# Attention in a fused two-layer encoder: scores with the sign turned, their minimum seeded with minus the sink, the sink as one more column under the exponential

## The chip, the cores and the metric

The kernel runs on one core of one Trainium2 chip. The time is the device time of one execution in microseconds (us), and of several runs the median is given. The engines are named as in the profile: PE is the matrix engine (PEld its weight loads), DVE the vector engine, ACT the scalar engine, POOL the GpSimd engine, SP the queue that issues the DMAs.

## What is computed

The reference is an encoder of two layers over two sequences, 256 and 512 tokens long, of width 1024. Layer 0 mixes tokens with an mLSTM, layer 1 with sliding-window attention; each is followed by a gated feed-forward with a short convolution. The part that matters here is the attention of layer 1: 16 query heads in 4 key/value groups, head width 64, query blocks of 128 and a window of 128 on each side, a bias per head that depends on the distance, and a learned sink per head, which takes part in the softmax as one more score without a value:

```python
s = einsum('bqkgd,bckd->bkgqc', qb, kb) * scale + bias
s = where(valid, s, -inf)
m = maximum(max(s, axis=-1, keepdims=True), sink)
p = exp(s - m)
denom = sum(p, axis=-1, keepdims=True) + exp(sink - m)
ob = einsum('bkgqc,bckd->bqkgd', p / denom, vb)
```

## The kernel before, in words

All 768 tokens lie side by side. A matrix product is made of three passes with operands split into a high and a low part (`whi`, `wlo` for weights, `zh`, `zl` for activations); ACT writes the high part (L259), DVE the low one (L260). Weights arrive by DMA in pieces of 512 KB into the tile `raw` (L268).

The attention is the function `swa`. First the keys and the first queries are projected (`window`), then the values (`gemmN`). `queries` (L876) takes a projected query tile out of the accumulator: ACT writes the high part times 0.125 (L887), DVE the low part (L888). The bias rows of all heads come from one small product; ACT copies it to the tile `bs` (L899), and it goes through memory (`brow`), from where each head's bias tile `bt` is fetched (L962).

Then comes the loop over 48 blocks (L1033). A block is one pair of heads by one query block of 128 rows; it sees two or three key tiles, K = 256 or 384 columns (32 blocks of the first kind, 16 of the second). Each step of the loop has four kinds of work:

- `project` (L915): a few matmuls of the remaining query projections, and later of the output projection, as filler;
- `scores` (L955) of block x: for each of the two heads (index e) PE multiplies queries and keys into an accumulator bank from the rotation `pa` of four; DVE adds the bias, writes the sum to the tile `t` and takes its maximum in the same instruction (L978). On 128x2 operands DVE then takes the maximum with the sink (L983), the sink minus that maximum (L984) and the negated maximum (L985). ACT makes the exponential of each head with its sum (L987), and the exponential of the sink's difference (L990). DVE adds the two (L991) and inverts the sum (L992); POOL multiplies the probabilities by the result (L994);
- `flip` (L996) of block x-3 (LAG is 3): PE transposes the probabilities into `pa` (L1002), ACT (L1006) and DVE (L1004) copy them to the tile `pt`;
- `values` (L1008), for three blocks at once: PE multiplies by the values, and when a sequence is complete the output is split into its two parts.

`t` has four buffers, `pt` five, `bt` three. The order on PE is as the loop is written (`manual_schedule` for PE alone, L1032). The order on DVE, ACT, POOL and SP is chosen when the program is built, by a timed model of the program; each engine then works through its queue in that order.

Of the kernel before, what the change touches and what calls it, by code (L numbers as in the profile page):

```python
# [10 lines left out]
F32 = mybir.dt.float32  # L11
R = mybir.dt.float32r
AF = mybir.ActivationFunctionType
ALU = mybir.AluOpType

P = 128
# [26 lines left out]
BIG = 1.0e30  # L43
# [9 lines left out]
SK = FG + 8  # L53
# [113 lines left out]
class Net:  # L167
# [679 lines left out]
    def swa(self, pool):  # L847
        nc, io = self.nc, self.io
# [27 lines left out]
        def queries(u, c):  # L876
            if c == 0:
                qts[u] = self.slab([P, 4, T], R)
            qt = qts[u]

            def evac(q, o):
                s0, s1 = SEQS[q]
                for e in range(2):
                    src = o[64 * e : 64 * e + 64]
                    hi = qt[64 * e : 64 * e + 64, 2 * c + e, s0:s1]
                    lo = qt[64 - 64 * e : 128 - 64 * e, 2 * c + e, s0:s1]
                    nc.scalar.activation(hi, src, AF.Copy, scale=0.125)  # L887
                    nc.vector.scalar_tensor_tensor(lo, src, 0.125, hi.bitcast(F32), ALU.mult, ALU.subtract)  # L888

            return evac  # L890

# [4 lines left out]
        pb = self.pa()[0:16]  # L896
        self.mm(pb, rb, oh, True, True)
        bs = pool.tile([16, 512], F32, tag="t", name="bs", bufs=4)
        nc.scalar.copy(bs, pb)  # L899

        bd = self.dp.tile([16, 512], F32, name="brow")
        nc.sync.dma_start(bd, bs)
# [39 lines left out]
        for j in range(8):  # L942
            for q, (s0, s1) in enumerate(SEQS):
                n = (s1 - s0) // P
                for i in range(n):
                    b = Block()
# [5 lines left out]
        bias = {}  # L952
        po = {}

        def scores(b):  # L955
            j, kv = b.j, b.j // 2
            if j not in bias:
                bias[j] = []
                for e in range(2):
                    bt = pool.tile([P, 384], F32, tag="bt", name=self.nm("bt"), bufs=3)  # L960
                    row = bd[2 * j + e : 2 * j + e + 1]
                    nc.sync.dma_start(  # L962
                        bt, bass.AP(tensor=row.tensor, offset=row.offset, ap=[[1, P], [1, 384]])
                    )
                    bias[j].append(bt)
            co = (b.lo - b.i + 1) * P
            k0 = b.s0 + b.lo * P
            q0 = b.s0 + b.i * P
            K = b.K
            b.t = t = pool.tile([P, 2, 384], F32, tag="t", name=self.nm("t"), bufs=4)  # L970
            st = pool.tile([P, 8], F32, tag="st", name=self.nm("st"), bufs=6)
            rm, mx, sm, rd = (st[:, 2 * z : 2 * z + 2] for z in range(4))
            for e in range(2):
                S = self.pa()[:, :K]
                qb = qts[j // 2][:, 2 * (j % 2) + e, q0 : q0 + P]
                for z in range(2):
                    self.mm(S, qb, kk[kv // 2][:, kv % 2, z, k0 : k0 + K], z == 0, z == 1)
                nc.vector.tensor_tensor_reduce(  # L978
                    out=t[:, e, :K], in0=S, in1=bias[j][e][:, 384 - co - K : 384 - co][:, ::-1], op0=ALU.add, op1=ALU.max,
                    scale=1.0, scalar=-BIG, accum_out=rm[:, e : e + 1],  # L980
                )
            sk = self.cst(SK + 2 * j, 2)
            nc.vector.tensor_tensor(mx, rm, sk, ALU.max)  # L983
            nc.vector.tensor_tensor(rd, sk, mx, ALU.subtract)  # L984
            nc.vector.tensor_scalar(mx, mx, -1.0, None, ALU.mult)  # L985
            for e in range(2):
                nc.scalar.activation(  # L987
                    t[:, e, :K], t[:, e, :K], AF.Exp, bias=mx[:, e : e + 1], accum_out=sm[:, e : e + 1]
                )
            nc.scalar.activation(rd, rd, AF.Exp)  # L990
            nc.vector.tensor_tensor(rd, rd, sm, ALU.add)  # L991
            nc.vector.reciprocal(rd, rd)  # L992
            for e in range(2):
                nc.gpsimd.tensor_scalar(t[:, e, :K], t[:, e, :K], rd[:, e : e + 1], 1.0, ALU.mult, ALU.mult)  # L994

# [36 lines left out]
        with self.tc.manual_schedule(engines={mybir.EngineType.PE}):  # L1032
            for x in range(nb + LAG + 1):  # L1033


                while done < min(113, AHEAD + (x + 1) * (113 - AHEAD) // 40) + max(0, 14 * (x - 40) // 10):
                    next(fill, None)
                    done += 1
                if x < nb:
                    scores(blocks[x])  # L1040
                if LAG <= x < nb + LAG:
                    flip(blocks[x - LAG])
                if x > LAG and (x - LAG) % GROUP == 0:
                    for b in blocks[x - LAG - GROUP : x - LAG]:
                        values(b)
# [620 lines left out]
```

## Time and profile before

| what | value |
|---|---|
| median of three timed runs | 1853.66 us (1852.61 to 1855.81) |
| span of the profiled execution, first to last instruction | 1851.5 us |
| total of the profiled execution beside its span | not listed; the median of the timed runs stands 2.16 us above the span |
| mean granted clock of PE over the span | 0.989 |
| DVE busy over the span | 1394.5 us (75%) |
| ACT busy over the span | 897.3 us (48%) |
| POOL busy over the span | 475.3 us (26%) |
| first and last bias-and-maximum on DVE (L978) | 1095.9 and 1237.9 us into the span |

Busy time says how long an engine had an instruction in work; it doesn't say that anybody waited for it. A view of waits names, for an engine that sat idle, what ended the idle time. The chain of work that ended last is followed back from the last instruction, so its shares tell what set the end. A view by windows gives the busy time of each engine in a stretch of the span, in the order PE, PEld, DVE, ACT, POOL, then the granted clock, the DMA share and the DMA rate.

### The profile page before, as it was taken

The page shows a single profiled execution, that of the slowest core. Times are in us where ns is not written, and L with a number is a line of the kernel's source. Part 1 is how long each engine was busy: PE and PEld are TensorE (multiplying, and loading weights), DVE is VectorE, ACT ScalarE, POOL GpSimd, SP SyncE. Part 2 cuts the span into 40 slices and gives each one's busy share as a digit, 9 for nine tenths or more (in the row PEclk, how much of TensorE's full clock was granted, in tenths as well). Part 3 has the DMA queues.
Part 4 walks back from the last instruction along what each step waited for, and adds up shares of the span by engine and source line. Part 5 has one row for each costly group of instructions (what it writes and reads, how often), then busy time and mean ns, then how long its engine had stood idle before and what let it go on. Part 6 is the DMA issues. An engine that isn't in the chain of part 4 may idle for free.

```text
span 1851.5 us, 29083 instructions
## 1 busy us (share of the span) xinstructions
PE 1799.6 (97%) x11290; PEld 1660.0 (90%) x11290; DVE 1394.5 (75%) x2292; ACT 897.3 (48%) x1815; POOL 475.3 (26%) x386
## 2 busy tenths in 40 slices
PE   6999999999999999999999999999999999999997
PEld 3987887888998999999999898889989999999997
DVE  4755676886689777777877858876898777777876
ACT  4444443443456444444444546765564444444443
POOL 1001001021024333333331313330134333333322
PEclk7999999999999999999999999999999999999999
DMA  8343556546312222222222321123122222222212
GB/s 329 117 147 132 174 190 223 168 139 201 106 46 80 69 69 69 68 69 69 68 69 83 104 82 49 52 94 121 51 92 69 69 69 69 69 69 69 69 35 69
DMA packets 64246, 184.49 MB, mean 100 GB/s; under 512 B 6167, under 2 KB 23831, under 8 KB 64108
## 3 DMA queue, kind: packets, MB, share of 16 engines
q1 hardware_dynamic: 64108, 182.63, 30.1%
q8 instruction: 89, 1.46, 0.3%
q14 instruction: 49, 0.40, 0.1%
HBM read 176.17 MB, written 6.43 MB: 99 GB/s over the span
## 4 chain that ended last, share of the span: by engine, by line
PE 86%; DVE 6%; DMA 3%; ACT 2%; issue 1%; POOL 1%; SPq 0%; POOLq 0%; ACTq 0%; DVEq 0%
PE ps L253 27%; PE pa L253 25%; PE ps L1163 10%; PE ps L1166 10%; PE ps L1164 10%; PE pa L1002 1%; DMA raw<-in_adaln_w_dram 1%; DVE wlo L260 1%; DMA raw<-in_w_dram 1%; DVE slab L589 1%; DMA slab<-in_adaln_w_dram 1%; PE pa L1166 0%; PE pa L1164 0%; PE pa L1163 0%; DMA slab<-mrows 0%
## 5 line engine op out<-in xcount | busy, mean ns | idle before, releaser
L259 ACT CAST whi<-raw 128x1024 fp32r<-128x1024 f32 x237 | 248.0, 1048 | 344.8 <-PE pa L253 162.0
L260 DVE TENSOR_TENSOR wlo<-raw,whi 128x1024 fp32r<-128x1024 f32 x237 | 322.3, 1361 | 113.7 <-ACT whi L259 111.7
L253 PE MATMUL pa<-slab,whi 128*128 128x256 f32 (+1 forms) x1472 | 346.5, 331 | 3.2 <-DVE slab L589 3.2
L253 PEld LDWEIGHTS pa<-slab,whi 128*128 128x128 f32 x1472 | 252.7, 188 | 27.5 <-DVE slab L589 4.6
L589 DVE SCALAR_TENSOR_TENSOR slab<-pa,mod,slab 128x256 f32<-128x256 f32 (+1 forms) x368 | 211.4, 593 | 69.6 <-PE pa L253 69.3
L253 PE MATMUL pa<-slab,wlo 128*128 128x256 f32 (+1 forms) x736 | 233.8, 330 | 0.0
L253 PE MATMUL ps<-zh,whi 128*128 128x256 f32 (+1 forms) x560 | 188.9, 338 | 2.3 <-ACT whi L259 1.7
L253 PE MATMUL ps<-zh,wlo 128*128 128x256 f32 (+1 forms) x560 | 184.1, 330 | 2.1 <-DVE wlo L260 2.1
L253 PE MATMUL ps<-zl,whi 128*128 128x256 f32 (+1 forms) x560 | 185.0, 332 | 0.0
L1163 PE MATMUL ps<-zh,whi 128*128 128x384 f32 x504 | 172.2, 342 | 3.7 <-ACT nt L1234 1.9
L1164 PE MATMUL ps<-zl,whi 128*128 128x384 f32 x504 | 169.9, 337 | 0.8 <-DVE zl L1120 0.8
L1166 PE MATMUL ps<-zh,wlo 128*128 128x384 f32 x504 | 168.9, 335 | 0.0
L253 PEld LDWEIGHTS pa<-slab,wlo 128*128 128x128 f32 x736 | 138.5, 188 | 13.1 <-DVE wlo L260 0.4
L1199 POOL TENSOR_TENSOR raw<-raw,raw 128x512 f32<-128x512 f32 x40 | 52.0, 1301 | 330.5 <-DVE wlo L260 246.1
L253 PE MATMUL ps<-slab,whi 128*128 128x384 f32 x512 | 132.2, 339 | 2.2 <-ACT sg L841 1.3
L1396 POOL TENSOR_TENSOR slab<-slab 128x772 f32<-128x772 f32 x44 | 86.5, 1967 | 171.5 <-DVE slab L1384 159.6
L1383 DVE SCALAR_TENSOR_TENSOR slab<-slab,cstt,slab 128x771 f32<-128x771 f32 x88 | 105.4, 1199 | 26.6 <-ACT slab L1381 26.4
L253 PEld LDWEIGHTS ps<-zh,whi 128*128 128x128 f32 x560 | 107.4, 192 | 15.9 <-issue 4.4
L505 DVE SCALAR_TENSOR_TENSOR ada<-raw,silc,ada 128x1024 f32<-128x1024 f32 x84 | 109.0, 1335 | 14.3 <-DMA raw<-in_adaln_w_dram 14.0
L253 PEld LDWEIGHTS ps<-zh,wlo 128*128 128x128 f32 x560 | 107.2, 192 | 12.4 <-DVE wlo L260 3.1
L253 PEld LDWEIGHTS ps<-zl,whi 128*128 128x128 f32 x560 | 107.2, 192 | 11.9 <-issue 3.4
L1196 POOL TENSOR_TENSOR raw<-raw 128x512 f32<-128x512 f32 x40 | 61.0, 1525 | 199.2 <-DMA raw<-in_w_dram 171.0
(294 smaller groups left out, 4303.0 us busy)
## 6 DMA issues: line engine op xcount, KB each, us to landing
raw<-in_w_dram SPq DMA_DIRECT2D x208, 512.0 KB, 3.7
raw<-in_adaln_w_dram SPq DMA_DIRECT2D x84, 512.0 KB, 4.6
slab<-in_x_dram SPq DMA_DIRECT2D x12, 512.0 KB, 7.1
slab<-in_adaln_w_dram SPq DMA_DIRECT2D x12, 512.0 KB, 10.3
slab<-mrows SPq DMA_DIRECT2D x8, 384.0 KB, 5.5
xs<-slab SPq DMA_DIRECT2D x6, 512.0 KB, 3.7
bt<-brow SPq DMA_DIRECT2D x16, 192.0 KB, 3.0
slab<-xs SPq DMA_DIRECT2D x6, 512.0 KB, 6.6
```

The source lines that it names most:

```text
L253: self.nc.tensor.matmul(out, lhsT, rhs, start=start, stop=stop)
L259: nc.scalar.copy(hi, src)
L260: return nc.vector.tensor_tensor(lo, src, hi.bitcast(F32), ALU.subtract)
L505: stt(acc[:, s], row, w, acc[:, s], ALU.mult, ALU.add)
L589: self.nc.vector.scalar_tensor_tensor(x, o, self.mod[l][:, gc + c, q : q + 1], x, ALU.mult, ALU.add)
L1163: mm(o, wh[:, k], hi[k], start=start and k == 0, stop=False, skip_group_check=True)
L1164: mm(o, wh[:, k], lo[k], start=False, stop=False, skip_group_check=True)
L1166: mm(o, wl[:, k], hi[k], start=False, stop=k == 3, skip_group_check=True)
L1196: tt(q[2], q[2], q[3], ALU.add)
L1199: tt(q[0], q[2], q[0], ALU.subtract)
L1383: stt(y[:, 1:], u[:, :-1], w(0), y[:, 1:], ALU.mult, ALU.add)
L1396: nc.gpsimd.tensor_tensor(y, y, yrow[:, j], ALU.mult)
```

## The change

The queries are scaled by -0.125 instead of 0.125, and the bias rows are negated as they are copied to `bs`, so every masked score comes out with the sign turned. A new tile `nsk` holds minus the sinks of all 16 heads; one DVE instruction fills it. The instruction that adds the bias now takes the minimum, and starts it from minus the sink of its head, read from `nsk` (before, it started from a constant). The result is minus the maximum that the softmax needs, so the three small DVE instructions go. `t` grows from 384 to 386 columns per head; ACT writes minus the sink into column K of both heads, and each exponential, with scale -1, runs over K + 1 columns. Its sum contains the sink's share, so the separate exponential and the addition go. Only the reciprocal is left of the small instructions.

```diff
-                    nc.scalar.activation(hi, src, AF.Copy, scale=0.125)
-                    nc.vector.scalar_tensor_tensor(lo, src, 0.125, hi.bitcast(F32), ALU.mult, ALU.subtract)
+                    nc.scalar.activation(hi, src, AF.Copy, scale=-0.125)
+                    nc.vector.scalar_tensor_tensor(lo, src, -0.125, hi.bitcast(F32), ALU.mult, ALU.subtract)
...
-        nc.scalar.copy(bs, pb)
+        nc.scalar.activation(bs, pb, AF.Copy, scale=-1.0)
+        nsk = pool.tile([P, 16], F32, name="nsk")
+        nc.vector.tensor_scalar(nsk, self.cst(SK, 16), -1.0, None, ALU.mult)
...
-            b.t = t = pool.tile([P, 2, 384], F32, tag="t", name=self.nm("t"), bufs=4)
-            st = pool.tile([P, 8], F32, tag="st", name=self.nm("st"), bufs=6)
-            rm, mx, sm, rd = (st[:, 2 * z : 2 * z + 2] for z in range(4))
+            b.t = t = pool.tile([P, 2, 386], F32, tag="t", name=self.nm("t"), bufs=4)
+            nc.scalar.copy(t[:, :, K : K + 1], nsk[:, 2 * j : 2 * j + 2].unsqueeze(2))
+            st = pool.tile([P, 6], F32, tag="st", name=self.nm("st"), bufs=6)
+            low, sm, rd = (st[:, 2 * z : 2 * z + 2] for z in range(3))
...
-                    out=t[:, e, :K], in0=S, in1=bias[j][e][:, 384 - co - K : 384 - co][:, ::-1], op0=ALU.add, op1=ALU.max,
-                    scale=1.0, scalar=-BIG, accum_out=rm[:, e : e + 1],
+                    out=t[:, e, :K], in0=S, in1=bias[j][e][:, 384 - co - K : 384 - co][:, ::-1], op0=ALU.add, op1=ALU.min,
+                    scale=1.0, scalar=nsk[:, 2 * j + e : 2 * j + e + 1], accum_out=low[:, e : e + 1],
                 )
-            sk = self.cst(SK + 2 * j, 2)
-            nc.vector.tensor_tensor(mx, rm, sk, ALU.max)
-            nc.vector.tensor_tensor(rd, sk, mx, ALU.subtract)
-            nc.vector.tensor_scalar(mx, mx, -1.0, None, ALU.mult)
             for e in range(2):
                 nc.scalar.activation(
-                    t[:, e, :K], t[:, e, :K], AF.Exp, bias=mx[:, e : e + 1], accum_out=sm[:, e : e + 1]
+                    t[:, e, : K + 1], t[:, e, : K + 1], AF.Exp, bias=low[:, e : e + 1], scale=-1.0,
+                    accum_out=sm[:, e : e + 1],
                 )
-            nc.scalar.activation(rd, rd, AF.Exp)
-            nc.vector.tensor_tensor(rd, rd, sm, ALU.add)
-            nc.vector.reciprocal(rd, rd)
+            nc.vector.reciprocal(rd, sm)
```

## The prediction

> **What bounds the kernel now.** The page's chain of the work that ended last comes first, because it tells which engine sets the end at all.
>
> ```profile
> PE 86%; DVE 6%; DMA 3%; ACT 2%; issue 1%; POOL 1%; SPq 0%; POOLq 0%; ACTq 0%; DVEq 0%
> ```
>
> PE holds 86% of it. Everything that the change takes away belongs to DVE and ACT, so it can shorten the run only where PE waits for those two. The change touches one stage, the 48 blocks of attention. I cut that stage by windows at the places where PE's busy time falls short of the stretch.
>
> ```profile
> 1095.00:1100.00 5.00, 5.00 (x38) 4.91 (x37) 3.91 (x15) 3.14 (x7) 0.00 (x0) 1.00 0.14 52
> 1100.00:1107.00 7.00, 5.50 (x33) 4.17 (x32) 6.34 (x32) 6.60 (x23) 2.82 (x6) 1.00 0.27 77
> 1107.00:1217.00 110.00, 109.99 (x920) 98.01 (x918) 94.90 (x387) 75.77 (x248) 35.37 (x71) 1.00 0.16 47
> 1217.00:1225.00 8.00, 5.61 (x39) 4.20 (x36) 6.67 (x31) 6.12 (x23) 2.08 (x4) 1.00 0.30 91
> 1225.00:1250.00 25.00, 24.46 (x227) 22.78 (x228) 15.03 (x69) 12.78 (x45) 7.89 (x16) 1.00 0.38 127
> ```
>
> The second number is the length, the third PE's busy time. In 110 us of the middle PE is busy for 109.99, though DVE is at 94.90 there: a crowded engine, but nobody on PE waits for it. PE's idle time is 1.50 us in the second row, 2.39 in the fourth, 0.54 in the last, 0.01 in the third: **4.44 us in all, and that is the ceiling** of what a faster softmax can bring here. PE's waits in the same stretch name what it waited for:
>
> ```profile
> PE pa L1002 <- POOL t L994: 1.9, 3, 1.2
> PE pa L1002 <- DVE st L983: 1.3, 1, 1.3
> PE ps L253 <- DVE slab L260: 0.5, 1, 0.5
> PE pa L1002 <- DVE pt L1004: 0.5, 1, 0.5
> ```
>
> Three of the four rows are transposes (L1002) that come before their probabilities are ready, or before a bank is free. The 0.5 us for L260 is the split of the last output, which the change doesn't touch.
>
> **The change part by part.** First the small instructions, counted in the stage (busy us, then mean ns):
>
> ```profile
> L984 DVE TENSOR_TENSOR st<-cstt,st 128x2 f32<-128x2 f32 x48 | 11.8, 246 | 1.1
> L985 DVE TENSOR_SCALAR st<-st 128x2 f32<-128x2 f32 x48 | 10.1, 209 | 0.9
> L983 DVE TENSOR_TENSOR st<-st,cstt 128x2 f32<-128x2 f32 x48 | 9.3, 194 | 0.1
> L991 DVE TENSOR_TENSOR st<-st 128x2 f32<-128x2 f32 x48 | 7.8, 163 | 7.9 <-ACT t L987 7.5
> L990 ACT ACTIVATE st<-st 128x2 f32<-128x2 f32 x48 | 9.6, 201 | 27.9 <-DVE st L984 27.6
> L987 ACT ACTIVATE t<-t,st 128x384 f32<-128x384 f32 x32 | 19.4, 611 | 0.6 <-DVE st L985 0.3
> ```
>
> Removed from DVE: 11.8 + 10.1 + 9.3 + 7.8 = 39.0 us busy. Removed from ACT: 9.6 us. Added to ACT: 48 copies of 128x2. No such copy is in the trace; the nearest row is the removed exponential itself, 201 ns on the same shape, so 48 x 0.20 = 9.6 us, and ACT comes out even (the bounds are nothing and 0.4 us each, twice the row; I take the row). The extra column is one element of 385: 611 / 384 = 1.6 ns at most, 96 times, 0.15 us.
>
> The minimum now starts from a value per partition. Whether that costs anything for this instruction no row shows, but another DVE instruction stands in the trace in both forms, with a column of values (L589) and with a constant (L263), on the same shape:
>
> ```profile
> L589 DVE SCALAR_TENSOR_TENSOR slab<-pa,mod,slab 128x512 f32<-128x512 f32 x160 | 116.5, 742 | 25.3 <-PE pa L253 25.3
> L263 DVE SCALAR_TENSOR_TENSOR slab<-ps,slab 128x512 fp32r<-128x512 f32 x8 | 5.5, 686 | 2.0 <-ACT slab L262 2.0
> ```
>
> 742 - 686 = 56 ns. I take that estimate, with nothing and twice that as bounds: 96 x 0.056 = 5.4 us on DVE. Net, DVE loses about 34 us of its 126.85 in the stage. Within the 110 us of the middle this is worth **nothing**, because PE already runs there without a wait. The cover for that statement is PE's own work; it would be gone only if a new wait came in (below).
>
> Once each, ahead of the loop: the fill of `nsk` (about 0.2 us on DVE, the row of L985) and the sign of `bs`, a copy that stays a copy. The first scores come tens of us behind them; DVE may hold PE up by that 0.2 us at most. The sign of the queries changes no instruction. The wider `t` puts the second head 8 bytes off its old place; no row isolates that, and I take nothing (bounds: 0.05 us either way per instruction, on engines with slack). No DMA is added, moved or resized.
>
> What is left is the two bubbles. The chain of work, read inside them, shows whose time they are. The first:
>
> ```profile
> 1100.56 0.16 DVE st L991
> 1100.72 0.07 DVE st L984
> ...
> 1101.34 0.07 DVE st L985
> ...
> 1101.74 0.30 DVE st L983
> ...
> 1102.38 0.11 DVE st L984
> ...
> 1103.63 0.07 DVE st L983
> 1103.70 0.09 DVE st L985
> ...
> 1105.13 0.59 POOL t L994
> ...
> 1105.76 0.55 PE pa L1002 x3
> ```
>
> All DVE rows here are instructions that go: 0.16 + 0.07 + 0.07 + 0.30 + 0.11 + 0.07 + 0.09 = 0.87 us. Four bias instructions stand between them and get longer: 4 x 0.056 = 0.22. Saved: 0.65 us. The second:
>
> ```profile
> 1218.56 0.07 DVE st L983
> 1218.63 0.07 DVE st L991
> ...
> 1219.65 0.07 DVE st L984
> ...
> 1221.54 0.17 DVE st L985
> ...
> 1222.04 0.07 DVE st L983
> ...
> 1222.45 0.07 DVE st L984
> 1222.53 0.46 DVE pt L1004
> 1222.99 0.15 DVE st L985
> 1223.14 0.07 DVE st L991
> ```
>
> The small ones are 0.74 us, less 0.22 for four longer bias instructions: 0.52. The copy L1004 (0.46) lies in this chain only because the negation that ACT waits for stands behind it in DVE's queue; without the negation ACT may start when the bias instruction ends. Saved: 0.98 us. Together **1.6 us**, to which the end of the stage adds nothing: its wait is for a split that stays. When the small instructions are gone, what is late next is DVE's long work in the same chain: weight splits, copies, the bias instructions.
>
> The profiled execution would go from 1851.5 us of span to 1849.9. Nothing outside the span changes. The median of the runs shown is 1853.66, 2.16 above that span, so the sum makes 1852.1.
>
> One rule speaks against reading PE's busy time as I did. The Trainium skill, page "Perfetto Trace Analysis", section "Identifying the Most-Contended Engine", holds matmul busy time to be a bad measure, since matmuls are pipelined, and would have the share of weight loads read instead. By it the middle stretch would have 110 - 98.01 = 12 us of room, and the sum could be 12 us lower; the trace speaks against it, since no wait of PE's falls into that stretch.
>
> **The rivals.** (1) *The bubbles stay.* The order on DVE and ACT is made anew by the builder's model, and a long instruction may again stand ahead of a late transpose. For it: the long rows in both chains remain. Against: DVE gets a quarter of its load off. Time: 1853.7, or a few us more with a new bubble of the size of the second (2.39).
>
> ```profile
> L978 DVE CUSTOM_DVE_ANT_0 t<-pa,bt x96: 404/425/560, 1095.9 to 1237.9; 128x256 f32<-128x256 f32 x64, 128x384 f32<-128x384 f32 x32
> ```
>
> (2) *Slower: ACT's copy waits for a buffer.* The copy is the first writer of a `t` buffer. There are four, so for block x it must wait until PE has transposed block x-4. Before, DVE's bias instruction was that writer, and its scores came from PE after those transposes anyway. Now the wait stands in ACT's in-order queue, and behind it are exponentials and the copies that free banks for PE. One block ahead it costs nothing. It decides from the point where the builder puts the copy three blocks ahead of an exponential: then each block must run, one after the other, PE's transposes, the copy 0.20, two exponentials with their sums 2 x 0.61 + 0.19, POOL's first head 0.59, transposes 2 x 0.55. With 0.16 for the reciprocal (as L991) that is 3.5 us, for three key tiles, against a pitch of 3.0 (the row above: 48 blocks from 1095.9 to 1237.9, 142 / 47). 16 such blocks x 0.45 = 7 us: 1861. For it: the copy waits for no scores, so it can be placed early. Against: a model that knows of the buffer would not place it there, and ACT has room (75.77 of 110).
>
> (3) *The change doesn't stop at the bubbles.* If PE in the middle is held by something that the waits don't show, 12 us more could go, as worked out above: 1840. Against it: 109.99 of 110.
>
> **How the numbers follow.** Forecast 0.55, alone 1849 to 1853.5 (between the ceiling and almost nothing). Rival (1) 0.18, rival (2) 0.22, rival (3) 0.05. About 0.2%, here 3.7 us, is what a measurement of this kernel can tell from no change. Faster by more: rival (3) and the part of the forecast in which nearly all 4.44 us go, 0.05 + 0.13 = 0.18. Slower by more: rival (2) and the worst of (1), 0.22 + 0.03 = 0.25. Within: 0.57. The range goes from the ceiling with the scatter of the runs (1853.66 - 4.44 - 1.2), 1848, up to rival (2) at 1861; it leaves out rival (3) and about half of (2), some 0.16.
>
> **What would show it.** Right: the middle of the stage as full on PE as before; DVE's busy time in the stage down by about 34 us with the run hardly shorter; the bias instruction's median near 480 ns (425 before); waits for L994 and for DVE at the transposes down from 3.7 us to about 2. Wrong: PE waits inside the middle stretch; ACT idle before the copy of the sink with PE's transposes named; bias instructions that wait for that copy; a bubble at the start or near the end longer than 2.4 us.

## The result, and the profile after

The changed kernel took 1847.27 us in the median of seven runs (1845.5 to 1852.27), the kernel before, run beside it, 1854.77 (seven runs, 1849.79 to 1857.39). The ratio is 0.9966, with a 95% interval from 0.9952 to 0.998. The gain is 7.5 us where I had 1.6, and by more than the 0.2% that a measurement of this kernel can tell from no change. My forecast of 1852.1 was 4.8 us too high, the time lies 0.7 us below my range, and to "faster by over 0.2%" I had given 0.18.

The profiled execution has a span of 1843.8 us instead of 1851.5. PE issues the same 11,290 matmuls in the same order in both kernels, so matmul n of one trace can be set against matmul n of the other, and the starts tell where the 7.7 us went, counted from the first matmul: 2.4 are gained ahead of the attention stage, 6.4 in it, 1.1 are given back at the start of the next feed-forward. In the twelve other kernels below, the part ahead of the stage differs from before by anything from -2.7 to +1.8 us, although their code there is the same but for a sign and the fill of `nsk`, so this part scatters (1.1 of the 2.4 us are one stretch at half clock, told in the last section). The given-back 1.1 us appears in eight of these twelve, the kernel that is slower than before among them, and follows no edit. The stage is what the change moves.

The chain of work that ended last has hardly changed: PE still holds 86% of it. For the windows I cut the stage of both kernels at the same matmuls, so that the rows can be subtracted: the first bubble, the middle, the second bubble, and a short rest that is left out here but is in the sum. The columns are those of the windows above. The kernel before:

```profile
1095.70:1107.63 11.93, 10.43 (x68) 8.98 (x66) 10.88 (x48) 9.94 (x28) 3.22 (x6) 1.00 0.18 52
1107.63:1216.99 109.36, 109.35 (x916) 97.50 (x915) 94.26 (x385) 75.52 (x247) 34.96 (x70) 1.00 0.16 47
1216.99:1226.60 9.61, 7.22 (x65) 5.64 (x63) 8.06 (x40) 7.30 (x27) 2.62 (x6) 1.00 0.25 76
...
sum 143.08, PE 139.18 PEld 123.64 DVE 123.06 ACT 100.23 POOL 46.29; mean PE 34.79 PEld 30.91 DVE 30.76 ACT 25.06 POOL 11.57
```

And the changed kernel:

```profile
1093.16:1103.37 10.21, 9.93 (x67) 8.99 (x66) 9.22 (x31) 9.88 (x26) 3.48 (x7) 1.00 0.14 38
1103.37:1210.42 107.05, 107.05 (x916) 97.14 (x915) 78.53 (x249) 75.19 (x251) 40.58 (x72) 1.00 0.17 51
1210.42:1217.73 7.31, 6.88 (x66) 5.77 (x64) 6.23 (x21) 6.00 (x24) 3.95 (x7) 1.00 0.34 100
...
sum 136.70, PE 135.99 PEld 123.45 DVE 102.74 ACT 99.64 POOL 52.32; mean PE 34.00 PEld 30.86 DVE 25.69 ACT 24.91 POOL 13.08
```

The bubbles lose 11.93 - 10.21 = 1.7 and 9.61 - 7.31 = 2.3 us. The middle, which I had left out of the sum, loses 109.36 - 107.05 = 2.3 us, although PE reads as busy for all of it in both kernels and does the same 916 matmuls. Weight loads take the same time too (97.50 and 97.14). Together with the short rest that is 6.4 us, more than the 4.44 us of PE idle time that I took for a ceiling.

PE's waits in the stage of the changed kernel (line waited for: us, times, longest):

```profile
PE ps L253 <- DVE slab L260: 0.5, 1, 0.5
PE pa L1000 <- DVE pt L1002: 0.3, 1, 0.3
PE pa L1000 <- DVE st L981: 0.2, 1, 0.2
```

The waits at the transposes (now L1000) have gone from 3.9 us to 0.5. (I had counted 3.7; the view before has one more row, of 0.2 us:)

```profile
PE pa L1002 <- DVE st L991: 0.2, 1, 0.2
```

The view of single lines for the two operations that the change adds or alters, the bias instruction (now L981) and the sink's copy (L973):

```profile
L981 DVE CUSTOM_DVE_ANT_0 t<-pa,bt,nsk x96: 465/484/620, 1093.4 to 1229.0; 128x256 f32<-128x256 f32 x64, 128x384 f32<-128x384 f32 x32
```

```profile
L973 ACT COPY t<-nsk x48: 177/183/197, 1060.2 to 1227.8; 128x2 f32<-128x2 f32 x48
```

The bias instruction's median went from 425 to 484 ns; the copy takes 183.

Last, a place where the mechanism can be read: the timeline of DVE and ACT around one block (start, duration, engine, line). Before:

```profile
1118.65 0.56 DVE L978 CUSTOM_DVE_ANT_0 t<-pa,bt 128x384 f32<-128x384 f32 x1
...
1119.13 0.55 DVE L978 CUSTOM_DVE_ANT_0 t<-pa,bt 128x384 f32<-128x384 f32 x1
...
1119.95 0.15 DVE L983 TENSOR_TENSOR st<-st,cstt 128x2 f32<-128x2 f32 x1
1120.14 0.16 DVE L991 TENSOR_TENSOR st<-st 128x2 f32<-128x2 f32 x1
1120.21 0.15 DVE L984 TENSOR_TENSOR st<-cstt,st 128x2 f32<-128x2 f32 x1
...
1120.80 0.50 DVE L985 TENSOR_SCALAR st<-st 128x2 f32<-128x2 f32 x1
...
1121.48 0.19 ACT L990 ACTIVATE st<-st 128x2 f32<-128x2 f32 x1
...
1121.83 0.62 ACT L987 ACTIVATE t<-t,st 128x384 f32<-128x384 f32 x1
...
1122.44 0.61 ACT L987 ACTIVATE t<-t,st 128x384 f32<-128x384 f32 x1
```

The two bias instructions end at 1119.21 and 1119.68. The maximum (L983) and the negation (L985) work on both heads at once, so they wait for both, and they stand in DVE's queue behind a copy, a bias instruction of another block and small steps. The first exponential starts 2.15 us after the second bias instruction's end. The last half microsecond of that passes in ACT's own queue, where a copy and the sink's exponential (L990, which also goes) stand ahead of it. The same in the changed kernel:

```profile
1113.98 0.62 DVE L981 CUSTOM_DVE_ANT_0 t<-pa,bt,nsk 128x384 f32<-128x384 f32 x1 [0.71 <-issue]
...
1114.60 0.60 DVE L981 CUSTOM_DVE_ANT_0 t<-pa,bt,nsk 128x384 f32<-128x384 f32 x1
1114.72 0.63 ACT L986 ACTIVATE t<-t,st 128x385 f32<-128x385 f32 x1
...
1115.42 0.62 ACT L986 ACTIVATE t<-t,st 128x385 f32<-128x385 f32 x1
```

The first head's exponential starts 0.12 us after its own bias instruction, while the second head's bias instruction still runs. Over the 48 blocks the mean delay from the end of the second bias instruction to the first exponential went from 1.96 us to -0.2, and to POOL's first multiplication from 4.10 to 1.84 us. That is more than the removed instructions last (1.0 us per block, by their mean durations in the prediction): the change takes away a meeting of the two heads and places in the queues.

### The profile page after: what moved, and what is told of

Read it like the earlier page. It is cut to its first block, busy times and chain, and to the rows that moved or that the text cites. A ratio compares the mean times of both kernels' runs of the same rounds, so it can differ in the third digit from the quotient of the medians.

```text
span 1843.8 us, 28933 instructions
## 1 busy us (share of the span) xinstructions
PE 1794.3 (97%) x11290; PEld 1657.0 (90%) x11290; DVE 1373.0 (74%) x2101; ACT 898.0 (49%) x1815; POOL 481.6 (26%) x386
## 4 chain that ended last, share of the span: by engine, by line
PE 86%; DVE 6%; DMA 3%; ACT 2%; issue 1%; POOL 1%; SPq 0%; POOLq 0%; ACTq 0%
PE ps L253 27%; PE pa L253 25%; PE ps L1161 10%; PE ps L1164 10%; PE ps L1162 10%; PE pa L1000 1%; DVE wlo L260 1%; DMA raw<-in_w_dram 1%; DMA slab<-in_x_dram 1%; DVE slab L589 1%; DMA slab<-in_adaln_w_dram 1%; DVE ada L505 0%; PE pa L1162 0%; PE pa L1164 0%; PE pa L1161 0%
## 5 line engine op out<-in xcount | busy, mean ns | idle before, releaser
L253 PE MATMUL pa<-slab,whi 128*128 128x256 f32 (+1 forms) x1472 | 346.5, 331 | 3.2 <-DVE slab L589 3.2
L253 PEld LDWEIGHTS pa<-slab,whi 128*128 128x128 f32 x1472 | 252.7, 188 | 27.6 <-DVE slab L589 4.7
L253 PE MATMUL pa<-slab,wlo 128*128 128x256 f32 (+1 forms) x736 | 233.8, 330 | 0.0
L253 PE MATMUL ps<-zh,whi 128*128 128x256 f32 (+1 forms) x560 | 188.9, 338 | 1.8 <-ACT whi L259 1.2
L253 PE MATMUL ps<-zh,wlo 128*128 128x256 f32 (+1 forms) x560 | 184.0, 330 | 1.4 <-DVE wlo L260 1.4
L253 PE MATMUL ps<-zl,whi 128*128 128x256 f32 (+1 forms) x560 | 184.9, 332 | 0.0
L253 PEld LDWEIGHTS pa<-slab,wlo 128*128 128x128 f32 x736 | 138.5, 188 | 13.1 <-DVE wlo L260 0.4
L253 PE MATMUL ps<-slab,whi 128*128 128x384 f32 x512 | 132.3, 339 | 2.2 <-ACT sg L841 1.3
L253 PEld LDWEIGHTS ps<-zh,whi 128*128 128x128 f32 x560 | 107.2, 192 | 15.1 <-issue 4.4
L253 PEld LDWEIGHTS ps<-zl,whi 128*128 128x128 f32 x560 | 107.3, 192 | 12.0 <-issue 3.4
L253 PEld LDWEIGHTS ps<-zh,wlo 128*128 128x128 f32 x560 | 107.2, 192 | 11.6 <-DVE wlo L260 2.3
```

What stands on the lines that cost most here:

```text
L253: self.nc.tensor.matmul(out, lhsT, rhs, start=start, stop=stop)
```

## The experiments

Three theories stood against each other. **Load:** DVE has less work, and everything that queues on it comes earlier. **Chain:** an exponential no longer waits for both heads and for small instructions in DVE's queue, and the reciprocal no longer waits for a separate exponential. **Scatter:** the gain lies outside the stage. By the comparison above the last can only be a minor part. My expectations give a stretch from the first to the last bias instruction (L978): 142.0 us before, 135.6 after the change.

In all kernels the order on PE is that of the loop; the orders on DVE, ACT and POOL are made anew at each build, so that an edit can also move neighbours. In the table "stage" is the difference from the profiled kernel before, by the same matmuls, and behind it the lengths of the first bubble, the middle and the second bubble; DVE is its busy time in the stage. The kernel before ran beside each group, at medians of 1853.47 to 1854.39 us.

| kernel | median us | ratio to before, 95% interval | stage us | bubble 1, middle, bubble 2 | DVE us |
|---|---|---|---|---|---|
| before | 1854.77 | 1 | 0 | 11.93, 109.36, 9.61 | 123.1 |
| changed | 1847.27 | 0.9966 (0.9952 to 0.998) | -6.4 | 10.21, 107.05, 7.31 | 102.7 |
| e1_pad | 1850.16 | 0.9975 (0.9965 to 0.9985) | -4.5 | 10.53, 107.30, 8.24 | 122.6 |
| e2_before_pt_act | 1850.02 | 0.998 (0.997 to 0.9989) | -3.3 | 11.60, 108.29, 7.78 | 105.5 |
| e3_min_only | 1849.57 | 0.9972 (0.9962 to 0.9982) | -4.3 | 10.92, 107.48, 8.27 | 111.9 |
| e4_column_only | 1849.78 | 0.9975 (0.9966 to 0.9984) | -3.8 | 10.63, 108.34, 8.19 | 108.0 |
| e5_const_seed | 1846.93 | 0.996 (0.9946 to 0.9973) | -6.8 | 10.09, 107.05, 6.99 | 97.6 |
| e6_recip_pool | 1846.73 | 0.9957 (0.9944 to 0.9969) | -6.7 | 10.04, 107.05, 7.18 | 98.6 |
| e7_after_pt_act | 1847.15 | 0.9958 (0.9946 to 0.9971) | -6.4 | 10.21, 107.06, 7.29 | 84.4 |
| e8_bank_hold | 1848.62 | 0.9968 (0.9956 to 0.9979) | -5.7 | 10.44, 107.05, 7.79 | 110.5 |
| e9_before_bank_hold | 1859.1 | 1.0031 (1.0019 to 1.0043) | +4.7 | 14.59, 109.58, 11.29 | 126.1 |
| e10_recip_pool_pt_act | 1848.98 | 0.997 (0.996 to 0.998) | -6.3 | 10.09, 107.03, 7.58 | 80.4 |
| e11_join | 1850.42 | 0.9978 (0.9969 to 0.9987) | -2.4 | 10.86, 109.93, 7.74 | 106.5 |
| e12_copy_unread | 1846.59 | 0.996 (0.9948 to 0.9973) | -5.9 | 10.40, 107.06, 7.58 | 106.7 |

### Load or chain

**e1_pad** gives the changed kernel DVE's old load back, without the old chain: four small instructions per block that nobody reads.

```diff
+            sk = self.cst(SK + 2 * j, 2)
+            pad = pool.tile([P, 6], F32, tag="pad", name=self.nm("pad"), bufs=6)
+            p0, p1, p2 = (pad[:, 2 * z : 2 * z + 2] for z in range(3))
+            nc.vector.tensor_tensor(p0, low, sk, ALU.max)
+            nc.vector.tensor_tensor(p1, sk, p0, ALU.subtract)
+            nc.vector.tensor_scalar(p0, p0, -1.0, None, ALU.mult)
...
+            nc.vector.tensor_tensor(p2, p1, sm, ALU.add)
             nc.vector.reciprocal(rd, sm)
```

> The changed kernel, with four DVE instructions on 128x2 put back per block, of the removed kinds and at their places in the program, into a scratch tile that nobody reads. Measured by the stretch from the first to the last bias instruction: 142.0 us before, 135.6 after the change. Theory A (the gain comes from DVE's shorter queue): about 39 us of work are back on DVE, so the stretch goes back to 140 to 143 us and the time to within 0.1% of before. Theory B (the gain comes from the shorter chain between DVE and ACT, since the exponentials wait for fewer steps): the chain stays short, stretch 135.5 to 137, ratio near 0.9966. Theory C (the gain is scatter outside the stage): the stretch as in B, but the ratio anywhere from 0.996 to 1.000.

Measured: 1850.16 us, 2.9 over the changed kernel and 4.0 under the kernel before. Its windows, cut at the same matmuls:

```profile
1098.09:1108.62 10.53, 9.94 (x67) 8.99 (x66) 9.67 (x40) 9.80 (x27) 2.75 (x6) 1.00 0.14 31
1108.62:1215.92 107.30, 107.30 (x917) 97.13 (x915) 94.21 (x393) 75.63 (x250) 35.44 (x71) 1.00 0.18 52
1215.92:1224.16 8.24, 7.30 (x65) 5.69 (x63) 7.53 (x34) 6.11 (x24) 3.76 (x8) 1.00 0.29 90
```

DVE is as busy in the middle as it was before (94.21 and 94.26 us), and yet the middle takes 107.30 us and not 109.36. Of the stage's 6.4 us, 4.5 stay. The stretch of the bias instructions is 137.7 us, between the 140 to 143 that I expected by the load and the 135.5 to 137 by the chain. So load alone doesn't explain the gain; it accounts for the 1.8 us that went, 1.2 of them in the bubbles.

**e11_join** does the reverse: it adds one small instruction per block, and both exponentials read its result. **e12_copy_unread** adds the same instruction and leaves the exponentials as they are (`bias=low`).

```diff
+            nc.vector.tensor_copy(both, low)
             for e in range(2):
                 nc.scalar.activation(
-                    t[:, e, : K + 1], t[:, e, : K + 1], AF.Exp, bias=low[:, e : e + 1], scale=-1.0,
+                    t[:, e, : K + 1], t[:, e, : K + 1], AF.Exp, bias=both[:, e : e + 1], scale=-1.0,
```

> The changed kernel with one more DVE instruction of 128x2 per block, a copy of both heads' minima, and both exponentials read the copy. So neither exponential can start before both bias instructions and one small instruction behind them in DVE's queue are done, as in the kernel before; the sink stays in the start value and in the column. If the gain is the chain (an exponential no longer waits for both heads and for a place in DVE's queue), the delay from the second bias instruction to the first exponential comes back to over 1 us (changed kernel: -0.2, before: 1.96), and the stage loses 1.5 to 3.5 of its 6.4 us: the middle takes 107.6 to 108.6 us instead of 107.05, median 1848.8 to 1850.8. If the gain is DVE's load, one small instruction is a quarter of the four that cost 1.8 us together: the stage loses 0.5 us, the middle takes 107.1, and this kernel and the next are alike.

> The same kernel with the same copy, but the exponentials read the minima themselves, as in the changed kernel; nobody reads the copy. The load on DVE is that of the kernel with the join, the chain is that of the changed kernel. By the chain the stage keeps 5.8 to 6.4 of its 6.4 us, the middle takes 107.05 to 107.15 us and the median is 1847.3 to 1848, which is 1.5 to 3 us under the kernel with the join. By the load both kernels come out the same, 0.5 us over the changed kernel.

Measured: 1850.42 us with the join and 1846.59 without, at the same load on DVE (106.5 and 106.7 us). The windows and PE's longest wait in the kernel with the join:

```profile
1094.67:1105.53 10.86, 10.01 (x67) 8.98 (x66) 9.55 (x34) 9.46 (x26) 3.35 (x5) 1.00 0.09 29
1105.53:1215.46 109.93, 108.99 (x916) 97.67 (x915) 81.00 (x284) 74.02 (x247) 35.93 (x72) 1.00 0.17 50
1215.46:1223.20 7.74, 7.02 (x66) 5.68 (x63) 6.70 (x25) 6.58 (x25) 3.01 (x6) 1.00 0.33 96
```

```profile
PE pa L253 <- DVE st L985: 0.7, 3, 0.3
```

and the middle of the kernel with the copy that nobody reads:

```profile
1104.97:1212.03 107.06, 107.06 (x917) 97.15 (x915) 81.33 (x285) 74.99 (x251) 40.60 (x72) 1.00 0.18 53
```

The pair tells load from chain. With the join the stage loses 3.9 of the 6.4 us, without it 0.5, and 0.5 is about a quarter of what four such instructions cost in e1_pad. The rest, 3.5 us, comes with the join. (The orders on DVE and ACT, made anew, differ between the two kernels as well; what a join costs in a fixed order no run here shows.) The delay to the first exponential is 1.27 us with the join and -0.24 without. The middle with the join is longer than I expected (109.93 us, not at most 108.6): it is 0.6 us worse than before, and part of it is now idle time of PE that shows, in score matmuls (L253) held by DVE's instruction at L985, the new copy.

### The two halves, and the queue alone

**e3_min_only** keeps the seeded minimum and goes back to a separate exponential for the sink; **e4_column_only** is the kernel before with the sink's column: the sign isn't turned, and DVE joins and negates the maximum as before. The cut of e3 is against the changed kernel, that of e4 against the kernel before.

```diff
e3
-            nc.scalar.copy(t[:, :, K : K + 1], nsk[:, 2 * j : 2 * j + 2].unsqueeze(2))
...
+            nc.vector.tensor_tensor(rd, low, nsk[:, 2 * j : 2 * j + 2], ALU.subtract)
...
+            nc.scalar.activation(rd, rd, AF.Exp)
+            nc.vector.tensor_tensor(rd, rd, sm, ALU.add)
...
e4
+            nc.scalar.copy(t[:, :, K : K + 1], self.cst(SK + 2 * j, 2).unsqueeze(2))
...
-            nc.vector.tensor_tensor(rd, sk, mx, ALU.subtract)
...
-            nc.scalar.activation(rd, rd, AF.Exp)
-            nc.vector.tensor_tensor(rd, rd, sm, ALU.add)
-            nc.vector.reciprocal(rd, rd)
+            nc.vector.reciprocal(rd, sm)
```

> Half of the change: the sign and the minimum that starts from minus the sink, but the sink's share by a subtraction on DVE, an exponential on ACT and an addition on DVE, as before. Two of the four small instructions go, the bias instructions get 56 ns longer: net 14 us less on DVE. Theory A: under half of the gain, stretch 138.5 to 140.5, ratio 0.998 to 0.9995. Theory B: the exponentials of the scores wait for the bias instruction alone unless ACT has the sink's exponential first, as it had before; then almost no gain, stretch 141 to 142.

> The other half: the maximum as before (maximum with the sink, negation), the sink as one more column under the exponential. Two of the four small instructions go and the bias instruction keeps its constant start: net 20 us less on DVE, and ACT loses the exponential that waited 27.6 us for DVE, for a copy that waits for nothing of DVE. Theory A: a little over half of the gain, stretch 137.5 to 139.5, ratio 0.9975 to 0.999. Theory B: the exponentials still wait for two small instructions, so less than half, stretch 139.5 to 141.

Measured: 1849.57 and 1849.78 us. The middle of e3_min_only:

```profile
1106.61:1214.09 107.48, 107.47 (x917) 97.13 (x915) 85.70 (x320) 75.83 (x249) 36.19 (x72) 1.00 0.17 50
```

and of e4_column_only:

```profile
1104.31:1212.65 108.34, 107.87 (x916) 97.26 (x915) 82.86 (x319) 75.95 (x254) 36.18 (x72) 1.00 0.18 52
```

Either half brings about two thirds of the stage's gain (4.3 and 3.8 of 6.4), so the two overlap. The stretches are 137.9 and 138.2 us: e3 gained more than either theory gave it, e4 came out as the load theory had it (137.5 to 139.5), so these totals don't decide. The two differ where the chain theory says that they should: with the seeded minimum the first exponential starts 0.20 us before the second bias instruction's end, and the middle is nearly as short as in the whole change, with more work on DVE (85.70 us against 82.86); with the column alone that delay is 1.66 us, and over half of the middle's gain is missing.

**e2_before_pt_act** leaves the kernel before as it is, but for the copy of the second head's transposed probabilities, which goes from DVE to ACT.

```diff
-                if e:
-                    nc.vector.tensor_copy(b.pt[:, e, : b.K], pp)
-                else:
-                    nc.scalar.copy(b.pt[:, e, : b.K], pp)
+                nc.scalar.copy(b.pt[:, e, : b.K], pp)
```

> The kernel before, with both copies of the transposed probabilities on ACT instead of one on ACT and one on DVE: 22 us of work leave DVE for ACT, and the softmax is untouched. Theory A: DVE is relieved by more than half of what the change relieved it, so the stretch of 142.0 us shrinks to 137 to 139.5 and the ratio is 0.997 to 0.9985. Theory B: nothing in the chain of the softmax gets shorter, stretch 141.5 to 143, ratio 0.9995 or more. Theory C: ratio 1.000 within 0.2%, whatever the stretch.

Measured: 1850.02 us; the middle:

```profile
1106.33:1214.62 108.29, 108.07 (x916) 97.15 (x915) 80.21 (x351) 86.80 (x282) 36.18 (x72) 1.00 0.17 48
```

DVE has 18 us less in the stage, about the relief that the change brings (20 us), and the stage gets 3.3 us shorter, half of the change's gain. The stretch is 138.7 us, which is what the load theory had said (137 to 139.5). So DVE's queue does have a price in the kernel before. The delay to the first exponential falls from 1.96 to 1.69 us, which fits a load that costs through the chain that queues behind it: then load and chain are not two sums that add. That reading is argued; no run separates it.

### What the added operations cost

**e5_const_seed** starts the minimum from a constant. The sink is left out of the minimum, and its column stays.

```diff
-                    scale=1.0, scalar=nsk[:, 2 * j + e : 2 * j + e + 1], accum_out=low[:, e : e + 1],
+                    scale=1.0, scalar=BIG, accum_out=low[:, e : e + 1],
```

> The changed kernel, with the minimum started from a constant instead of minus the sink; the sink is left out of the minimum, and stays the extra column. It measures the price of the start value per partition by itself. The bias instruction's median should go from 484 ns back to 425. If that price matters by its sum (5.4 us on DVE), the stretch from the first to the last bias instruction goes from 135.6 us to about 135.2 at the rate that the padded kernel showed (1.8 us of the stage for 39 us of DVE work); if the bias instruction is the step that PE waits for at each block, 2 x 59 ns in some of the 48 blocks: 133 to 135. Ratio 0.9955 to 0.9966.

Measured: 1846.93 us. The bias instruction is back at its old duration:

```profile
L981 DVE CUSTOM_DVE_ANT_0 t<-pa,bt x96: 404/425/560, 1094.8 to 1229.9; 128x256 f32<-128x256 f32 x64, 128x384 f32<-128x384 f32 x32
```

The value per partition costs 484 - 425 = 59 ns for each instruction, 5.7 us of DVE in 96, and 0.4 us of the stage, nearly all of it in the bubbles. The medians (1846.93 and 1847.27) can't be told apart. Of the two expectations, the price by its sum held: the stretch is 135.1 us.

### Is the middle at its floor?

Three kernels take more off DVE: **e6_recip_pool** has POOL make the reciprocal (as a power of -1), **e7_after_pt_act** is the changed kernel with the edit of e2_before_pt_act, and **e10_recip_pool_pt_act** has both. **e8_bank_hold** adds to DVE, ahead of each bias instruction, a small one that reads the same score bank and that nobody needs.

```diff
e6
+        mone = pool.tile([P, 2], F32, name="mone")
+        nc.vector.memset(mone, -1.0)
...
-            nc.vector.reciprocal(rd, sm)
+            nc.gpsimd.tensor_tensor(rd, sm, mone, ALU.pow)
...
e8
+            pad = pool.tile([P, 4], F32, tag="pad", name=self.nm("pad"), bufs=6)
...
+                nc.vector.tensor_scalar(pad[:, 2 * e : 2 * e + 2], S[:, :2], 1.0, None, ALU.add)
```

> The changed kernel, with the reciprocal on POOL (a power of -1 on 128x2) instead of DVE. DVE then never waits for ACT's sums inside a block (8.9 us of idle time in 16 waits after the change), and POOL gets about 0.7 us more per block. Theory A (DVE's load): 7.8 us less, stretch 135.2 from 135.6. Theory B (what stands in DVE's queue behind a wait for ACT): bias instructions come sooner, stretch 134 to 135. Against both: the chain to the transposes gets 0.5 us longer per block; if that is late anywhere, 136 to 138 and waits for POOL at the transposes.

> The changed kernel, with both copies of the transposed probabilities on ACT: 22 us leave DVE. Theory A: the stretch shrinks from 135.6 us to 134 to 135, since the same move on the kernel before brought 3.3 us of the stage. Theory B: the chain is short already and only a little is left, while ACT gets 22 us more and its exponentials come later: 135.5 to 137, with ACT named in the waits. Ratio to before 0.9955 to 0.997.

> The changed kernel with both reliefs of DVE together: the reciprocal by POOL (power of -1), and both copies of the transposed probabilities by ACT. DVE loses about 4 and 18 us of its 103 us in the stage. If the stage is at PE's floor but for the two bubbles, nothing is left to take beyond them: the middle 107.05 us again, the stage shorter than the changed kernel's by 0 to 1.1 us (bubble 1 has 0.28 us of PE idle time left, bubble 2 0.43), median 1846 to 1847. If DVE's load still priced the stage at the rate that the padded kernel showed (1.8 us for 20 us), 22 us less would bring 2 us: 1845.3, with a middle below 107.

> The changed kernel, with one more DVE instruction per head, on 128x2, that reads the bank of the scores ahead of the bias instruction (its result is not used). It holds every score bank some 0.1 to 0.16 us longer and puts 96 x 0.16 = 15 us on DVE. Theory A and a load rate of 1.8 us for 39 us: stretch 136.3. If PE waits for these banks in steps too short to show (the hidden waits in the middle of the stage), the stretch grows by 2 to 6 us, to 137.5 to 141.5, while the middle still reads as full on PE with no wait named. If the banks have slack: 135.6 to 136.3.

Measured: 1846.73, 1847.15, 1848.98 and 1848.62 us. The middle of e10_recip_pool_pt_act, which has the least work on DVE:

```profile
1107.76:1214.79 107.03, 107.03 (x916) 97.10 (x915) 60.46 (x179) 84.82 (x286) 65.75 (x108) 1.00 0.17 51
```

and of e8_bank_hold:

```profile
1103.83:1210.88 107.05, 107.05 (x917) 97.14 (x915) 84.32 (x318) 75.73 (x250) 35.01 (x71) 1.00 0.17 51
```

Whether DVE is busy for 60, 79 or 84 us there, the middle takes 107.03 to 107.06 us. I read that as PE's own time for these matmuls; the kernel before was 2.3 us above it, the changed kernel stands on it. A lighter DVE brought nothing beyond 0.3 us in the bubbles (0.4 with the shorter bias instruction of e5_const_seed), and none of the four can be told from the changed kernel by its median. By their stretches (135.3 and 136.3 us) e6 and e8 cost what the load theory had said, and e7 (135.6 us) gained nothing. (The stage of e10_recip_pool_pt_act is 0.1 us longer than the changed kernel's; its span, 1847.6 us, and with it the median over the 1846 to 1847 that I expected, comes from the scattering part ahead of the stage.) The span of e8_bank_hold, 1848.4 us, is longer mostly for what lies behind the stage: 3.8 us are lost in the last feed-forward, where PE ran at half clock for 10.2 us.

### What held the middle before

If PE was held in the middle while it read as busy, the starts of matmuls must show it. Matmul by matmul, 2.05 of the 2.3 us come from 22 of 916 starts, in six places, by 0.08 to 0.17 us each: 12 starts of score matmuls (1.2 us) and 10 of the transposes behind them (0.8 us). The timeline of PE at the first of them, before (four score matmuls, then four transposes):

```profile
1119.43 0.83 PE L253 MATMUL pa<-slab,slab 128*128 128x256 f32 x4
1120.18 0.74 PE L1002 MATMUL pa<-kct,t 128*128 128x128 f32 x4
```

and the same eight in the changed kernel:

```profile
1115.19 0.64 PE L253 MATMUL pa<-slab,slab 128*128 128x256 f32 x4
1115.67 0.60 PE L1000 MATMUL pa<-kct,t 128*128 128x128 f32 x4
```

The four scores take 0.83 us instead of 0.64, because the third and the fourth start 0.20 and 0.22 us after the one ahead instead of 0.12. At that moment the bias instruction of 1119.13 in the timeline above ends (1119.68), and with it a score bank comes free; the third score starts at 1119.75. No idle time is recorded, since the matmul ahead is booked as lasting 0.28 us, over the next one's start: a wait of 0.1 us vanishes under it. The late start of the fourth has no wait of its own on record; at all six places it follows a held third, by about 0.10 us more than without. The first and the third transpose start at 1120.18 and 1120.50, just after the copies of DVE (to 1120.03) and ACT (to 1120.36) out of `pa` have ended, which fits banks that came free late there too.

DVE's own rows tell what stood ahead of the late bias instruction of 1119.13:

```profile
1116.46 0.16 DVE L991 TENSOR_TENSOR st<-st 128x2 f32<-128x2 f32 x1 [0.52 <-ACT t L987]
...
1118.15 0.15 DVE L983 TENSOR_TENSOR st<-st,cstt 128x2 f32<-128x2 f32 x1
...
1118.53 0.17 DVE L985 TENSOR_SCALAR st<-st 128x2 f32<-128x2 f32 x1
```

DVE had waited 0.52 us for an exponential, and from there it worked without a pause of over 0.05 us. The same wait and the same unbroken run stand ahead of all six places, and at five of them the three removed instructions L983 to L985 take 0.5 us of the run (here from 1118.15 to the bias instruction of 1118.65).

The same starts in the other kernels: with e11_join the third score is late at all six places again (0.26 to 0.54 us behind the second), with e12_copy_unread it is at 0.12 us everywhere. So at equal load the join brings the held scores back. But e2, e3 and e4 have them at 0.12 us too, though in e2 and e4 the exponentials still wait for both heads. What is left of the middle there (1.2 and 1.3 us) lies mostly in late starts of transposes, 0.7 and 1.0 us.

**e9_before_bank_hold** puts the edit of e8_bank_hold into the kernel before, to let the banks go later still.

> The kernel before, with one unread DVE instruction of 128x2 ahead of each bias instruction, which reads the score bank, so that each bank is let go later by some 0.08 us. It adds work that nothing uses; the result is as before. In the changed kernel the same edit cost nothing in the middle of the attention stage (107.05 us for the same matmuls with and without). If the middle before the change was held by late score banks that the waits don't show, the same matmuls (109.4 us before) now take 1 to 4 us more, while PE still reads as busy for all but 0.3 us of them, and the score matmuls at the six places start as far apart as before (0.20 to 0.22 us) or further. If the middle was PE's own time, as I predicted, they take 109.4 us again, within 0.2, as the edit does in the changed kernel. Median about 1855 to 1858 by the first, 1854 by the second.

Measured: 1859.1 us, 5.6 over the kernel before. Its windows, PE's longest wait in the stage, and the timeline at the same eight matmuls:

```profile
1096.85:1111.44 14.59, 11.56 (x68) 10.13 (x66) 11.22 (x59) 10.04 (x28) 4.07 (x6) 0.88 0.14 48
1111.44:1221.02 109.58, 109.42 (x917) 97.70 (x915) 95.94 (x454) 76.09 (x247) 34.97 (x70) 1.00 0.17 47
1221.02:1232.31 11.29, 8.54 (x66) 6.88 (x64) 8.85 (x47) 8.07 (x30) 3.57 (x8) 0.85 0.24 67
```

```profile
PE pa L1004 <- POOL t L996: 5.2, 3, 3.0
```

```profile
1123.27 0.96 PE L253 MATMUL pa<-slab,slab 128*128 128x256 f32 x4
1124.15 0.65 PE L1004 MATMUL pa<-kct,t 128*128 128x128 f32 x4
```

My expectation of 1 to 4 us in the middle fell: it grew by 0.2, which is what I had written for a middle that is PE's own time. Taken alone, this length speaks against the held banks. The scores do start later (0.96 us for the four instead of 0.83, and so at five of the six places), which fits banks that come free late; but the transposes behind them then find theirs ready (0.65 instead of 0.74), and most of it is made good. The time of this kernel went elsewhere: the bubbles grew by 2.7 and 1.7 us, with POOL's multiplication up to 3.0 us late. Of that, 1.5 and 0.4 us are idle time of PE; the rest is busy time, and in each of the two bubbles PE ran at half clock for 3.4 us. So the held starts are shown in the matmul records, and that the join brings them back. That the score banks hold them rests on the times at which bias instructions end; the one run that held the banks longer moved the starts, but not the sum.

## Why the prediction was wrong

**The failed step** is "Within the 110 us of the middle this is worth **nothing**, because PE already runs there without a wait." The middle gave 2.3 us: 22 matmuls started 0.08 to 0.17 us late, scores behind bias instructions that came late in DVE's queue, and the transposes after them. PE's busy time in a window, and the view of waits, didn't show them, since the matmul ahead is booked over the next one's start; the comparison of starts does. With that step fell the ceiling of 4.44 us, which was the sum of the idle time that shows.

**The bubbles** were mis-sized: 0.65 and 0.98 us expected, 1.7 and 2.3 measured. I had added up the pieces of removed instructions in the chain of waits (and had counted four bias instructions in the first chain, which has three: 0.70 instead of 0.65). That prices their work, not the meeting of the two heads and the places in the queues. What made the bubbles' 4.0 us piece by piece stays open: the old load on DVE brings 1.2 of them back (e1_pad), the join 0.6 beyond its load (e11_join against e12_copy_unread). The join's other 2.9 us lie in the middle.

**The rivals.** (3), that PE in the middle is held by something that the waits don't show, was right in kind, and I gave it 0.05. The Trainium skill's page "Perfetto Trace Analysis", section "Identifying the Most-Contended Engine", holds matmul busy time to be a bad measure; I set that aside because no wait fell into the stretch. The trace bears it out: 109.35 of 109.36 us busy, and 2.3 of them to be saved. The share of weight loads, which the rule would have read instead, would have misled as far the other way: it left 12 us of room, and at 107.05 us, under which a lighter DVE got by 0.02 at most, weight loads still read 97.14. (2), that ACT's copy waits for a buffer, is refuted: ACT's only idle time in front of the copy is 0.2 us, once, for the bias rows' trip through memory. (1), that the bubbles stay, is refuted too: of PE's idle time there, 3.9 us before, 0.7 is left.

**What was right:** the value per partition costs 59 ns (56 estimated from rows of another instruction with another output type, so the closeness is partly luck); ACT comes out even (100.23 and 99.64 us busy); the copy costs nothing on the path; and the wait at the end of the stage stays at 0.5 us. DVE's busy time fell by 20.3 us where I had 34: I had added the durations of small instructions, and these overlap their neighbours (in the timeline before, the maximum of 1119.95 starts while the copy ahead of it, 0.42 us from 1119.61, is still running). e1_pad shows the same: its 192 small instructions last 35.8 us by sum and raise DVE's busy time by 19.8.

## What to carry to other kernels

Price a removed instruction between two engines by what its result waited for, not by its duration: the same small copy cost 0.5 us when nobody read it and 3.9 when both exponentials waited for it. A matrix engine that reads as full may still be held in short pieces, so before you write "no gain here", compare the distances from start to start of like matmuls (0.12 us against 0.20 to 0.22 here): waits of 0.1 us left no idle time in these traces. A test that adds the same instruction twice, once with a reader and once without, separates load from chain.

## What the hardware showed beside it

After one and the same wait of PE the granted clock fell to half for different lengths of time, or not at all. Just ahead of the attention stage PE waits 2.2 us in all fourteen kernels (the row is from the view of waits of the changed kernel):

```profile
PE pa L253 <- DVE zl L551: 2.2, 1, 2.2
```

The windows at and behind that wait, before:

```profile
1060.00:1065.00 5.00, 3.23 (x15) 3.23 (x16) 4.89 (x11) 3.48 (x7) 0.00 (x0) 0.58 0.10 25
1065.00:1070.00 5.00, 5.00 (x34) 5.00 (x34) 2.32 (x4) 1.09 (x2) 0.00 (x0) 0.74 0.32 103
```

and in the changed kernel:

```profile
1060.00:1065.00 5.00, 4.70 (x26) 4.70 (x27) 4.89 (x11) 2.56 (x8) 0.00 (x0) 0.66 0.38 104
1065.00:1070.00 5.00, 5.00 (x44) 5.00 (x43) 3.33 (x6) 3.49 (x7) 0.00 (x0) 1.00 0.16 33
```

With the same wait go 6.8 us at half clock in the one run and 3.4 in the other, which is 1.1 us of the measured difference. It follows no edit: 6.8 us are also in e1, e3, e6, e10 and e11, 3.4 in e2, e5, e7, e8, e9 and e12, and in e4_column_only, with the same wait, the clock stayed full:

```profile
1060.00:1065.00 5.00, 2.83 (x23) 2.68 (x23) 4.86 (x11) 3.95 (x13) 0.00 (x0) 1.00 0.04 10
```

In e9_before_bank_hold a wait of 3.0 us in the first bubble was followed by 3.4 us at half clock (the granted clock was 0.50 from 1106.5 to 1109.0 us), and equal matmuls started 0.43 us apart instead of 0.23. In its second bubble the clock fell for another 3.4 us within a wait of 1.5 us, while the waits of at most 1.3 us in the bubbles of the kernel before left the clock at 1.00. The Trainium skill's page "TensorE: Matmul & The Clock Gate", section "Part 1: The HAM clock gate", gives a window of about 3.4 us for both directions. The lengths of the slow stretches agree with it (3.4, 6.8 and 10.2 us are what these traces show); that a full idle window is needed doesn't, since the clock fell with waits of 2.2 and 1.5 us. What decides whether a wait is followed by half clock, no run here shows.
